# S5 set-up and S5 scans of a hybrid encoder trunk: POOL's share given to DVE, smaller steps, another place for the squares of a norm

## The chip, the cores and the metric

The kernel runs on one core of a Trainium2 chip. The metric is device time in microseconds (us) of one execution, here the median of three runs. The engines are called PE (TensorE, matmuls; PEld are its weight loads), DVE (VectorE), ACT (ScalarE), POOL (GpSimd) and SP (SyncE, which only issues DMAs). Each takes its instructions in order; they meet through semaphores.

## The reference, cut to what matters

The program is a trunk of two layers over 512 tokens of width 1024, all in f32. Layer 0 mixes with RWKV-7 and Mamba-2, layer 1 with an S5 state-space model and an mLSTM, and each layer ends with a squared-ReLU MLP. The change lies in S5, and in what runs beside it. Of S5, per direction, group and state:

```python
dt = exp(log_dt); mag = exp(dt * ar)
abr, abi = mag * cos(dt * ai), mag * sin(dt * ai)        # complex decay of a step
bur = einsum("bsgm,gpm->bsgp", ud, bbr); bui = ...       # inputs, complex
x_t = (abr + i abi) * x_(t-1) + (bur_t + i bui_t)        # a scan over time
yd  = einsum(xr, C_re) - einsum(xi, C_im)
y   = gelu(y); y * sigmoid(y @ glu_w + glu_b)
```

The norm in question is the plain one ahead of layer 1's mixers, `x * rsqrt(mean(x * x) + eps) * w`.

## The kernel before, in words

Every large product is done as three f32r matmuls (`mm3`, `project`, lines 99 to 101 and 112 to 114): the weights come by DMA into `wraw` (SP queue, line 86), ACT rounds them into `whi` (line 87), DVE takes the rest as `wlo` (line 88), and a product of 128 rows over 1024 inputs is 24 matmuls of 512 columns. `wraw`, `whi` and `wlo` have two buffers each, and the PSUM tag `mm` has two banks, so weights are ready at most two products ahead and a third product waits until the bank of the first has been read.

**The MLP of layer 0 and what runs beside it.** `mlp` makes 64 such tiles: 10 up, 8 down, 8 up, 8 down, 8 up, 8 down, 6 up, 8 down. An up tile is evacuated by ACT (`hid`, line 219), POOL and DVE (lines 223 and 224), a down tile by DVE (`evac`, line 251) and POOL (the add into `x`, line 253). After each tile `beside()` takes one turn of a generator, `S5.params`, and ties its instructions behind the tile's last DVE instruction (`issue_after`). So a turn of `params` that puts many instructions on DVE stands between the evacuation of one tile and the `wlo` of a later one.

`params` computes in turn 48 the decay of eight steps as a magnitude and a unit complex number (`unit`, `square`), and from it by repeated squaring its powers 1, 2, 4, 8, 16 and 32; then the tables `cos` and `sin` (128 x 32 groups x 64 chunks): in round i, k = 2^i new columns are the k first ones times a power, by a complex product `cmul` (lines 1455 to 1460, six elementwise instructions: DVE has three, POOL the other three when it is passed as `eng2`, and DVE all six when it isn't). Before, turns 48 and 49 hold three and five squares, turn 50 the rounds k = 1, 2, 4, 8, turn 51 k = 16, turns 52 and 53 the halves of k = 32, turn 54 a copy of `sin` with the sign turned (ACT, line 1599). Turns 43 to 50 are down tiles, 51 to 56 up tiles, 57 to 64 down tiles.

**The norm ahead of layer 1.** `rms_scale` calls `mean_square`: ACT squares the eight `x` (line 140, three buffers `sq`), POOL adds them one by one (line 145, six adds, `sqa`), PE sums over partitions with a matrix of ones (lines 148 and 149). Pools are stacks on two sides of SBUF. On the right, `pre1` (three `sq`, two `sqa`, one `ms`, 2 KB each) lies behind `xn1` and, of the MLP's memory, on tiles of `act0` that are read by matmuls alone. On the left it comes behind `ml_c` and `io_1`, 21,280 bytes in from where the MLP's pool `io0` began (3 `sq`, 2 `sqa`, `ms`, `rstd`, 2 `hid`, 2 `hid2`, 2 `evac` of 2 KB, in this order): its `sq` buffers then lie on the second `hid2` and on both `evac`, its `sqa` and `ms` on `act0`. After `pre1` the pool `s5_a` (S5's matrices `s5_m`, its inputs `s5_ul`) is opened on the right.

**The S5 scans.** PE's order is written by hand here (`manual_schedule`); for the other engines a planner orders the instructions by its own estimate of their times. First come the four S5 columns (written to DRAM as `s5_ud` and read back transposed as `s5_ul`, line 1622, eight DMAs), then the column of the mLSTM's gates, then `dense_steps(S5_STEPS[0])`, a turn of the gates, `dense_steps(S5_STEPS[1])`, and then the turns of `scan` with `S5_STEPS[2]` dense steps after each, and from turn `S5_STEPS[3]` on a turn of the gates too. The gates have 14 turns. A dense step is one k of a projection, three matmuls; sixteen projections of eight steps are in the chain: three `values` (their `wlo` on DVE), eight gated ones (`wlo`, line 88, and a product, line 1101, on POOL), five `values`. For each of four quarters `scan` does, twice, 8 matmuls of 64 columns into a bank `mix0`, two DVE products with `cos` and `sin` (lines 1638, 1639) and a POOL add (line 1640); then four scans on DVE (lines 1643, 1645); then the rotation back: two DVE products, two POOL memsets (lines 1649, 1650), a DVE and a POOL subtraction (lines 1651, 1652).

Of the kernel before, what the change touches and what calls it, by code (L numbers as in the profile page):

```python
# [14 lines left out]
ALU = mybir.AluOpType  # L15
# [251 lines left out]
PREP = (2, 3)  # L267
SPLIT = 6
END = (4, 24)
S5_STEPS = 4, 2, 7, 2, 3  # L270
OUT_STEPS = (0,) * 10 + (0, 1, 1) * 11 + (0,) * 8
NA = 2
DECAY = float(np.exp(-0.5))
# [1055 lines left out]
class S5:  # L1329
# [16 lines left out]
    def params(self, kp, tp):  # L1346
# [226 lines left out]
        def square(o, x, two=2.0):  # L1573
            tt(zq, x, x, M)
            stt(o[:, 1], x[:, 0], two, x[:, 1], M, M)
            tt(o[:, 0], zq[:, 0], zq[:, 1], Sb)
            unit(o)

        unit(z[0])
        square(z[6], z[0])  # L1580
        square(z[0], z[6])
        square(z[1], z[0], sgn)
        yield
        for i in range(1, 6):
            square(z[i + 1], z[i])
        yield

        tr, ti = self.cos, self.sin[:, 0]
        nc.gpsimd.memset(tr[:, :, 0:1], 1.0)
        nc.gpsimd.memset(ti[:, :, 0:1], 0.0)  # L1590
        for i in range(6):
            k = 1 << i
            for G in ([slice(0, 32)] if k < 32 else [slice(0, 16), slice(16, 32)]):
                n = G.stop - G.start
                b = lambda x: z[i + 1][:, x, G].unsqueeze(2).to_broadcast([128, n, k])
                cmul(tr[:, G, k:2 * k], ti[:, G, k:2 * k], tr[:, G, 0:k], ti[:, G, 0:k], b(0), b(1), (128, n, k), nc.gpsimd)
                if k >= 8:
                    yield
        nc.scalar.activation(self.sin[:, 1], ti, AF.Copy, scale=-1.0)
        yield  # L1600
# [15 lines left out]
    def scan(self, kp, wp):  # L1616

        c, nc = self.c, self.c.nc
        self.ul = ul = kp.tile([128, 32, 64], F32, tag="s5_ul", name="s5_ul")
        us = self.ud.rearrange("i (g m) j c -> j m (i g) c", m=16)  # L1620
        for j in range(8):
            nc.sync.dma_start(ul[16 * j:16 * j + 16], us[j])  # L1622
        self.inputs(kp, 6)
        lo, hi = slice(0, 64), slice(64, 128)
        self.X = X = self.sin
        flat = lambda x: x.rearrange("p g c -> p (g c)")
        M = ALU.mult
        for q in range(4):
            G = slice(8 * q, 8 * q + 8)
            w, t = (c.tile(wp, [128, 2, 8, 64], "s5_" + n, 2) for n in ("w", "t"))  # L1630
            for i in (0, 1):
                ps = c.bank("mix0", 2)
                pv = ps.rearrange("p (x g c) -> p x g c", x=2, g=4)
                for x in (0, 1):
                    for g in range(4):
                        nc.tensor.matmul(pv[:, x, g], lhsT=self.mats[2 * q + i][:, g, x], rhs=ul[:, 8 * q + 4 * i + g], start=True, stop=True)
                H, F = slice(4 * i, 4 * i + 4), slice(8 * q + 4 * i, 8 * q + 4 * i + 4)
                nc.vector.tensor_tensor(out=w[:, :, H], in0=pv, in1=self.cos[:, F].unsqueeze(1).to_broadcast([128, 2, 4, 64]), op=M)
                nc.vector.tensor_tensor(out=t[:, :, H], in0=pv[:, ::-1], in1=self.sin[:, :, F], op=M)
                nc.gpsimd.tensor_tensor(out=w[:, :, H], in0=w[:, :, H], in1=t[:, :, H], op=ALU.add)  # L1640
                yield
            for x in (0, 1):
                nc.vector.tensor_tensor_scan(flat(w[lo, x]), flat(self.rc[lo, G]), flat(w[lo, x]), 0.0, M, ALU.add)  # L1643
                rv = lambda v: flat(v)[:, ::-1]
                nc.vector.tensor_tensor_scan(rv(w[hi, x]), rv(self.rc[hi, G]), rv(w[hi, x]), 0.0, M, ALU.add)  # L1645
            t = c.tile(wp, [128, 2, 8, 64], "s5_t", 2)
            nc.vector.tensor_tensor(out=t, in0=w[:, ::-1], in1=self.sin[:, :, G], op=M)
            nc.vector.tensor_tensor(out=w, in0=w, in1=self.cos[:, G].unsqueeze(1).to_broadcast([128, 2, 8, 64]), op=M)
            nc.gpsimd.memset(X[lo, :, G, 0:1], 0.0)
            nc.gpsimd.memset(X[hi, :, G, 63:64], 0.0)  # L1650
            nc.vector.tensor_tensor(out=X[lo, :, G, 1:64], in0=w[lo, :, :, 0:63], in1=t[lo, :, :, 0:63], op=ALU.subtract)
            nc.gpsimd.tensor_tensor(out=X[hi, :, G, 0:63], in0=w[hi, :, :, 1:64], in1=t[hi, :, :, 1:64], op=ALU.subtract)
            yield

    def outputs(self, kp):
# [98 lines left out]
def trunk(tc, ap, out):  # L1754
    nc = tc.nc
    with ExitStack() as ctx:
# [130 lines left out]
        with ExitStack() as left:  # L1887
            s5k = left.enter_context(pool("s5_k"))

            with pool("s5_t", "right") as tp:  # L1890
                feed_forward(X, 0, s5.params(s5k, tp))
            mlc = left.enter_context(pool("ml_c"))
            ml = Mlstm(c, mlc)
            io = left.enter_context(pool("io_1"))
            c.io = io
            w_in = ap["cd_in"]
            with ExitStack() as right:
                xnp = right.enter_context(pool("xn1", "right"))
                with pool("pre1", "right") as pre:
                    c.io = pre  # L1900
                    xn = [c.split(x, xnp, 8, mix_w[1][:, k:k + 1]) for k, x in enumerate(X)]
                    rstd = c.rms_scale(X, io)
                c.io = io
                sa = right.enter_context(pool("s5_a", "right"))
                column = lambda i, use, eng=None: c.project(w_in[i], 128, xn, lambda ps: use(ps, rstd), eng)
                values = [column(4 + i, lambda ps, r, i=i: ml.values(i, ps, r)) for i in range(8)]
                gated = [column(12 + i, lambda ps, r, i=i: ml.outgate(i, ps, r), nc.gpsimd) for i in range(8)]
                dense = chain(values[:3] + gated + values[3:])
                left_over = 128

                def dense_steps(n):
                    nonlocal left_over
                    left_over -= n
                    for _ in range(n):
                        next(dense, None)

                with tc.manual_schedule(engines={nc.tensor.engine}):
                    s5.inputs(sa, 2)
                    for i in range(4):
                        drain(column(i, lambda ps, r, i=i: s5.columns(i, ps, r)))  # L1920
                    with pool("s5_w") as sw, pool("ml_t") as tp:
                        gates = []
                        drain(column(20, lambda ps, r: gates.append(ml.gates(ps, r, tp))))
                        gates, scan = gates[0], s5.scan(sa, sw)
                        next(gates)
                        dense_steps(S5_STEPS[0])
                        next(gates)
                        dense_steps(S5_STEPS[1])

                        for i, _ in enumerate(scan):  # L1930
                            dense_steps(S5_STEPS[2])
                            if i >= S5_STEPS[3]:
                                next(gates, None)
                        for _ in gates:
                            dense_steps(S5_STEPS[4])
                    pools = [left.enter_context(pool("ml_h0"))]
                    heads = [ml.head(h, pools) for h in range(8)]
                    dense_steps(7)
                    together((s5.outputs(sa), 5), (chain(islice(h, FRONT) for h in heads[:AHEAD_HEADS]), FRONT * AHEAD_HEADS), (dense, left_over))
            with pool("mix1", "right") as mixp, pool("ml_y", "right") as yp, pool("ml_h1") as hp:  # L1940
                pools.append(hp)
                y, mixed = [], []

                def beside_heads():
                    for t in s5.finish(yp, s5_vec):
                        mixed.append(c.split(t, mixp, 4))
                        yield
                    yield from project_out(c, X, ap["cd_out_a"], mixed)
                    yield from project_out(c, X, ap["cd_out_b"], y[:4], 0)

                side = beside_heads()
                for i in range(10):
                    for h, n in ((i - 1, 1), (i, 0), (i - 2, 2)):
                        if 0 <= h < 8 and (n or h >= AHEAD_HEADS):
                            for _ in range((FRONT, MIDDLE, 1)[n]):
                                t = next(heads[h])
                            if n == 2:
                                y.append(c.split(t, yp, 8))
                    for _ in range(BESIDE[i]):
                        next(side, None)  # L1960
                drain(side)
                drain(project_out(c, X, ap["cd_out_b"], y[4:], 4))
# [50 lines left out]
```

## Time and profile before

| | us |
|---|---|
| runs | 1829.66, 1825.49, 1831.63 (median 1829.66) |
| profiled execution | 1829.6 |
| its span | 1827.5 |
| PE busy | 1694.1 (93%) |
| DVE busy | 1182.1 (65%) |
| ACT busy | 733.2 (40%) |
| POOL busy | 584.6 (32%) |
| mean granted TensorE clock | 0.973 |

All times within the execution count from the start of the span. A granted clock of 1.00 is 2.4 GHz, and half of it is 1.2 GHz; a matmul of 512 columns starts every 0.23 us at the first and every 0.43 us at the second. Of the work that concerns us, the MLP of layer 0 ends at about 1048 us, the norm of layer 1 at 1067 us, and the S5 scans and the gates fill 1085 to 1213 us. In a timeline row the last bracket is the idle time of the engine just before the instruction and what ended it. "Busy" of DVE and POOL holds the time in which an instruction that has begun waits for the other of the two.

### The profile page before, as it was taken

To read this page: it belongs to the slowest core of one execution; us is meant where nothing else is said; L and a number is where in the kernel's file an instruction comes from. 1 tells how busy PE (TensorE), PEld (TensorE's weight loads), DVE (VectorE), ACT (ScalarE), POOL (GpSimd) and SP (SyncE) were. 2 spreads that over 40 slices of the span, in tenths; PEclk is the share of its full clock that TensorE was granted. 3 is DMA by queue.
4 is the path that set the end of the run, shared out by engine and by line. 5 is a ranking of instruction groups with operands and counts; after the bars stand their busy time and mean duration, and the time that the engine had idled before them with its cause. 6 is when DMAs were issued, how large, how long until landed. Compare 5 with 4: busy or idle time off the path is not lost. (4 is left out here: it accounts for less than half of the span.)

```text
span 1827.5 us, 26365 instructions
## 1 busy us (share of the span) xinstructions
PE 1694.1 (93%) x10124; PEld 1349.3 (74%) x10124; DVE 1182.1 (65%) x2051; ACT 733.2 (40%) x1262; POOL 584.6 (32%) x569
## 2 busy tenths in 40 slices
PE   7989989899899999999996978699889999999997
PEld 5777767687578787777775857578667788888887
DVE  6879796976876476656566657943657745353555
ACT  5635354433634343232322323144756532323243
POOL 4312121300641225566535224530121222222222
PEclk9999999999999999999998998889989999999999
DMA  4230202124302323334351364254222232333342
GB/s 164 79 93 21 65 22 79 30 70 134 121 18 77 93 93 102 105 116 139 106 160 46 113 171 159 87 192 136 86 77 63 87 99 92 103 94 94 102 130 68
DMA packets 90046, 177.40 MB, mean 97 GB/s; under 512 B 32688, under 2 KB 39600, under 8 KB 89792
## 3 DMA queue, kind: packets, MB, share of 16 engines
q1 hardware_dynamic: 82176, 157.32, 28.2%
q0 software_dynamic: 3200, 11.05, 1.8%
q10 hardware_dynamic: 4544, 7.34, 1.1%
q8 instruction: 80, 1.31, 0.3%
q14 instruction: 46, 0.38, 0.1%
HBM read 149.24 MB, written 28.54 MB: 97 GB/s over the span
## 5 line engine op out<-in xcount | busy, mean ns | idle before, releaser
L101 PE MATMUL mm<-act,wlo 128*128 128x512 f32 (+1 forms) x1264 | 483.8, 383 | 15.6 <-DVE wlo L88 15.2
L99 PE MATMUL mm<-act,whi 128*128 128x512 f32 (+1 forms) x1264 | 485.7, 385 | 12.1 <-ACT hid L219 3.1
L100 PE MATMUL mm<-act,whi 128*128 128x512 f32 (+1 forms) x1264 | 482.4, 382 | 0.7 <-DVE act L126 0.5
L87 ACT ACTIVATE whi<-wraw 128x1024 fp32r<-128x1024 f32 (+1 forms) x230 | 227.4, 989 | 561.2 <-PE mm L100 434.2
L88 DVE TENSOR_TENSOR wlo<-wraw,whi 128x1024 fp32r<-128x1024 f32 (+1 forms) x222 | 309.7, 1395 | 166.1 <-ACT whi L87 162.9
L101 PEld LDWEIGHTS mm<-act,wlo 128*128 128x128 f32 x1264 | 239.3, 189 | 66.4 <-DVE wlo L88 21.5
L99 PEld LDWEIGHTS mm<-act,whi 128*128 128x128 f32 x1264 | 239.1, 189 | 62.4 <-ACT hid L219 4.4
L100 PEld LDWEIGHTS mm<-act,whi 128*128 128x128 f32 x1264 | 239.5, 189 | 47.4 <-DVE act L126 1.4
L114 PE MATMUL mm<-act,wlo 128*128 128x512 f32 (+1 forms) x464 | 188.5, 406 | 23.5 <-POOL wlo L88 18.1
L112 PE MATMUL mm<-act,whi 128*128 128x512 f32 (+1 forms) x464 | 205.3, 442 | 3.4 <-DVE pad L77 1.8
L113 PE MATMUL mm<-act,whi 128*128 128x512 f32 (+1 forms) x464 | 186.7, 402 | 0.0
L223 POOL TENSOR_TENSOR hid<-hid 128x512 f32<-128x512 f32 x64 | 94.2, 1473 | 224.8 <-ACT hid L219 220.4
L253 POOL TENSOR_TENSOR x<-x,evac 128x512 f32<-128x512 f32 x56 | 77.7, 1388 | 192.4 <-DVE evac L251 184.4
L114 PEld LDWEIGHTS mm<-act,wlo 128*128 128x128 f32 (+1 forms) x464 | 89.2, 192 | 49.2 <-POOL wlo L88 20.7
L251 DVE TENSOR_TENSOR evac<-mm,rstd 128x512 f32<-128x512 f32 (+1 forms) x72 | 45.3, 629 | 115.9 <-PE mm L101 115.8
L112 PEld LDWEIGHTS mm<-act,whi 128*128 128x128 f32 (+1 forms) x464 | 89.3, 193 | 29.4 <-issue 5.6
L113 PEld LDWEIGHTS mm<-act,whi 128*128 128x128 f32 (+1 forms) x464 | 89.6, 193 | 15.6 <-issue 1.7
L224 DVE TENSOR_TENSOR act<-hid,act 128x512 fp32r<-128x512 f32 x64 | 46.5, 726 | 61.0 <-POOL hid L223 61.0
L77 DVE TENSOR_TENSOR pad<-mm,rstd 128x512 f32<-128x512 f32 x32 | 21.9, 684 | 49.1 <-PE mm L114 49.1
L145 POOL TENSOR_TENSOR sqa<-sqa,sq 128x512 f32<-128x512 f32 (+1 forms) x30 | 38.8, 1294 | 45.1 <-ACT sq L140 43.1
L76 POOL MEMSET pad<- 128x2 f32 x34 | 3.4, 105 | 154.6 <-DVE sh L768 55.3
L1750 DVE TENSOR_TENSOR x<-mm,x 128x512 f32<-128x512 f32 x32 | 22.1, 690 | 40.8 <-PE mm L101 40.8
(561 smaller groups left out, 2876.9 us busy)
## 6 DMA issues: line engine op xcount, KB each, us to landing
wraw<-mlp_w SPq DMA_DIRECT2D x130, 512.0 KB, 3.5
wraw<-ab_in SPq DMA_DIRECT2D x34, 512.0 KB, 3.6
wraw<-cd_in SPq DMA_DIRECT2D x21, 512.0 KB, 3.6
x<-x SPq DMA_DIRECT2D x16, 256.0 KB, 4.4
wraw<-ab_out_b SPq DMA_DIRECT2D x8, 512.0 KB, 3.5
s_cm<-s_sin POOLq DMA_DIRECT2D x8, 512.0 KB, 5.1
s_bm<-s_bt POOLq DMA_DIRECT2D x8, 512.0 KB, 5.0
s_m<-s_bm SPq DMA_DIRECT2D x8, 512.0 KB, 6.2
```

Source lines behind the costliest of these rows:

```text
L87: nc.scalar.activation(hi[:, :cols], raw[:, :cols], AF.Copy)
L88: (eng or nc.vector).tensor_tensor(out=lo[:, :cols], in0=raw[:, :cols], in1=hi[:, :cols].bitcast(F32), op=ALU.subtract)
L99: nc.tensor.matmul(out, lhsT=wh, rhs=xh, start=start and k == 0, stop=False)
L100: nc.tensor.matmul(out, lhsT=wh, rhs=xl, start=False, stop=False)
L101: nc.tensor.matmul(out, lhsT=wl, rhs=xh, start=False, stop=stop and k == n - 1)
L112: nc.tensor.matmul(out, lhsT=wh, rhs=xh, start=k == 0, stop=False)
L113: nc.tensor.matmul(out, lhsT=wh, rhs=xl, start=False, stop=False)
L114: nc.tensor.matmul(out, lhsT=wl, rhs=xh, start=False, stop=k == len(xs) - 1)
L223: nc.gpsimd.tensor_tensor(out=sq, in0=h, in1=h, op=ALU.mult)
L224: last[0] = nc.vector.tensor_tensor(out=lo, in0=sq, in1=hi.bitcast(F32), op=ALU.subtract)
L251: last[0] = nc.vector.tensor_tensor(out=t, in0=ps, in1=r2[:, a:b], op=ALU.mult)
L253: (nc.vector if b - a < T else nc.gpsimd).tensor_tensor(out=x, in0=x, in1=t, op=ALU.add)
```

## The change

Five edits: (1) the chain of squares in `params` gives up its turn five times instead of two; (2) the tables are made by DVE alone, in pieces of at most 256 elements a partition, with a turn after each piece from k = 4 on; (3) in `scan` the adds, one of the two subtractions and the memsets go from POOL to DVE, and there is a turn after each pair of scans, so 20 turns instead of 12; (4) `S5_STEPS` goes with it; (5) `pre1` is opened on the left.

```diff
-S5_STEPS = 4, 2, 7, 2, 3
+S5_STEPS = 8, 8, 4, 4, 3
 ...
         unit(z[0])
         square(z[6], z[0])
+        yield
         square(z[0], z[6])
         square(z[1], z[0], sgn)
         yield
         for i in range(1, 6):
             square(z[i + 1], z[i])
-        yield
+            if i % 2:
+                yield
 ...
             k = 1 << i
-            for G in ([slice(0, 32)] if k < 32 else [slice(0, 16), slice(16, 32)]):
-                n = G.stop - G.start
+            n = min(32, 256 // k)
+            for G in (slice(g, g + n) for g in range(0, 32, n)):
                 b = lambda x: z[i + 1][:, x, G].unsqueeze(2).to_broadcast([128, n, k])
-                cmul(tr[:, G, k:2 * k], ti[:, G, k:2 * k], tr[:, G, 0:k], ti[:, G, 0:k], b(0), b(1), (128, n, k), nc.gpsimd)
-                if k >= 8:
+                cmul(tr[:, G, k:2 * k], ti[:, G, k:2 * k], tr[:, G, 0:k], ti[:, G, 0:k], b(0), b(1), (128, n, k))
+                if k >= 4:
                     yield
 ...
-                nc.gpsimd.tensor_tensor(out=w[:, :, H], in0=w[:, :, H], in1=t[:, :, H], op=ALU.add)
+                nc.vector.tensor_tensor(out=w[:, :, H], in0=w[:, :, H], in1=t[:, :, H], op=ALU.add)
                 yield
             for x in (0, 1):
                 ...
                 nc.vector.tensor_tensor_scan(rv(w[hi, x]), rv(self.rc[hi, G]), rv(w[hi, x]), 0.0, M, ALU.add)
+                yield
 ...
-            nc.gpsimd.memset(X[lo, :, G, 0:1], 0.0)
-            nc.gpsimd.memset(X[hi, :, G, 63:64], 0.0)
+            nc.vector.memset(X[lo, :, G, 0:1], 0.0)
+            nc.vector.memset(X[hi, :, G, 63:64], 0.0)
             nc.vector.tensor_tensor(out=X[lo, :, G, 1:64], in0=w[lo, :, :, 0:63], in1=t[lo, :, :, 0:63], op=ALU.subtract)
-            nc.gpsimd.tensor_tensor(out=X[hi, :, G, 0:63], in0=w[hi, :, :, 1:64], in1=t[hi, :, :, 1:64], op=ALU.subtract)
+            nc.vector.tensor_tensor(out=X[hi, :, G, 0:63], in0=w[hi, :, :, 1:64], in1=t[hi, :, :, 1:64], op=ALU.subtract)
 ...
-                with pool("pre1", "right") as pre:
+                with pool("pre1") as pre:
```

After it the turns of `params` are: 48 and 49 one square (with what came before it) and two; 50, 51 and 52 one, two and two; 53 the rounds k = 1, 2 and 4; 54 k = 8; 55 and 56 the halves of k = 16; 57 to 60 the quarters of k = 32; 61 the copy on ACT. Before, 6 dense steps stand ahead of the scans, 84 among them, 6 in the gates' last turns; after, 16, 80 and none. Both then have 7 dense steps ahead of S5's outputs.

## Rows read from the trace of the kernel before

**Rows 1.** Busy time by stretch: length, PE, PEld, DVE, ACT, POOL, clock, DMA share, GB/s.
```profile
650.00:660.00 10.00, 10.00 (x46) 8.29 (x45) 9.32 (x34) 3.47 (x7) 2.08 (x2) 1.00 0.20 68
700.00:710.00 10.00, 8.00 (x23) 6.34 (x24) 4.77 (x6) 0.25 (x1) 4.30 (x3) 0.66 0.31 107
937.00:1010.00 73.00, 53.75 (x217) 42.36 (x217) 49.41 (x104) 19.50 (x23) 32.38 (x33) 0.91 0.25 79
1085.00:1213.00 128.00, 95.72 (x439) 75.59 (x438) 96.83 (x109) 34.38 (x45) 62.28 (x41) 0.87 0.45 133
```

**Rows 2.** Timeline of DVE, down tiles: start, length, line, operation, [idle before].
```profile
937.32 0.69 DVE L251 TENSOR_TENSOR evac<-mm,rstd 128x512 f32<-128x512 f32 x1 [2.30 <-PE mm L101]
...
1010.30 0.69 DVE L251 TENSOR_TENSOR evac<-mm,rstd 128x512 f32<-128x512 f32 x1 [1.90 <-PE mm L101]
1011.17 2.28 DVE L88 TENSOR_TENSOR wlo<-wraw,whi 128x1024 fp32r<-128x1024 f32 x1 [0.18 <-ACT whi L87]
...
1015.74 0.69 DVE L251 TENSOR_TENSOR evac<-mm,rstd 128x512 f32<-128x512 f32 x1 [1.62 <-PE mm L101]
```

**Rows 3.** Timeline of DVE, the first instruction of two squares that follow each other.
```profile
953.41 0.23 DVE L1376 TENSOR_TENSOR s_zq<-s_z 128x64 f32<-128x64 f32 x1
...
954.86 0.23 DVE L1376 TENSOR_TENSOR s_zq<-s_z 128x64 f32<-128x64 f32 x1
```

**Rows 4.** Timeline of DVE, products of the tables: with 256 and with 512 elements.
```profile
981.45 0.41 DVE L1459 TENSOR_TENSOR s_sin<-s_sin,s_z 128x256 f32<-128x256 f32 x1
...
988.81 0.69 DVE L1459 TENSOR_TENSOR s_sin<-s_sin,s_z 128x512 f32<-128x512 f32 x1 [1.15 <-POOL s_sin L1460]
989.42 1.53 DVE L1455 TENSOR_TENSOR s_sin<-s_cos,s_z 128x512 f32<-128x512 f32 x1
```

**Rows 5.** Timeline of DVE and PE around a `cmul` of 512 elements on DVE alone.
```profile
696.62 0.68 DVE L1455 TENSOR_TENSOR s_sin<-s_fr,c_s_bc 128x512 f32<-128x512 f32 x1
...
700.73 1.22 DVE L88 TENSOR_TENSOR wlo<-wraw,whi 128x1024 fp32r<-128x1024 f32 x1
...
702.00 0.80 PE L101 MATMUL mm<-act,wlo 128*128 128x512 f32 x1 [3.25 <-DVE wlo L88]
```

**Rows 6.** Timeline of ACT and POOL at the norm of layer 1.
```profile
1051.11 0.62 ACT L140 ACTIVATE sq<-x 128x512 f32<-128x512 f32 x1
...
1049.15 1.30 POOL L253 TENSOR_TENSOR x<-x,evac 128x512 f32<-128x512 f32 x1 [3.98 <-DVE evac L251]
...
1050.48 2.21 POOL L145 TENSOR_TENSOR sqa<-sq,sq 128x512 f32<-128x512 f32 x1
1052.76 7.00 POOL L145 TENSOR_TENSOR sqa<-sqa,sq 128x512 f32<-128x512 f32 x5
```

**Rows 7.** Timeline of SP, ACT and PE ahead of the first scan.
```profile
1085.17 9.62 SPq L1622 DMA_DIRECT2D s_ul<-s_ud  x8
1094.89 1.59 SPq L86 DMA_DIRECT2D wraw<-cd_in  x2
...
1101.58 1.06 ACT L87 ACTIVATE whi<-wraw 128x1024 fp32r<-128x1024 f32 x1 [10.63 <-DMA wraw<-cd_in]
...
1100.59 3.65 PE L1636 MATMUL mix<-s_ul,s_m 128*128 128x64 f32 x16 [9.74 <-DMA s_ul<-s_ud]
```

**Rows 8.** Waits, 1085 to 1213: who for whom, us in total, times, longest.
```profile
PE mm L114 <- POOL wlo L88: 18.1, 6, 7.4
```

**Rows 9.** Groups on POOL, 1085 to 1213: count, busy, mean ns, idle before, releasers.
```profile
L1652 POOL TENSOR_TENSOR s_sin<-s_w,s_t 64x1008 f32<-64x1008 f32 x4 | 13.2, 3297 | 2.7 <-DVE ml_small L1157 1.6 <-DVE s_w L1648 1.0
...
L1640 POOL TENSOR_TENSOR s_w<-s_w,s_t 128x512 f32<-128x512 f32 x8 | 12.1, 1514 | 27.7 <-DVE s_t L1639 26.1 <-DVE ml_small L1154 1.5
...
L1649 POOL MEMSET s_sin<- 64x16 f32 x4 | 0.5, 121 | 17.7 <-DVE s_t L1647 10.3 <-DVE ml_small L1154 7.4
```

**Rows 10.** DVE's own subtraction: its group of four, and one that began ahead of POOL's.
```profile
L1651 DVE TENSOR_TENSOR s_sin<-s_w,s_t 64x1008 f32<-64x1008 f32 x4 | 10.9, 2730 | 0.1
...
1207.40 1.20 DVE L1651 TENSOR_TENSOR s_sin<-s_w,s_t 64x1008 f32<-64x1008 f32 x1
```

## The prediction

> **What bounds the kernel now.** I read busy time by stretch first. PE is the engine that everything waits for, so what counts is where it stands still or runs at half clock. Two stretches touch the change. From 937 to 1010 PE is busy 53.75 of 73.00 us at a granted clock of 0.91: 19.25 idle, and 53.75 x 0.09 = 4.8 lost to the clock, 24.0 together. From 1085 to 1213 it is busy 95.72 of 128.00 at 0.87: 32.3 idle and 12.4 of clock, 44.7 together [rows 1]. The timeline of DVE gives the first number once more: from the evacuation at 937.32 (turn 48) to that at 1010.30 (turn 57) there are nine tiles, and one takes 1015.74 - 1010.30 = 5.44 us, so 72.98 - 48.96 = 24.0 [rows 2]. Then the waits and the timelines say who is late: in the first stretch DVE, which holds the squares and half of the tables in front of `evac` and `wlo`; in the second, S5's inputs, for which PE stands still 9.74 us ahead of the first scan matmul [rows 7], and POOL, on whose `wlo` PE waits 18.1 us in six waits [rows 8].
>
> The sum is made against the profiled execution, 1829.6 us (span 1827.5 and 2.1 around it); the median of the runs is 1829.66, so it holds for both.
>
> **Squares and tables (edits 1 and 2).** Removed: nine squares in two turns, and products on two engines that hinder each other. A DVE product of 512 elements takes 0.69 us alone and 1.53 beside POOL's [rows 4]. Added: POOL's three products of each `cmul` on DVE. With 256 elements one takes 0.41 us and the next begins 0.33 later [rows 4], so a piece is at most 6 x 0.41 = 2.5 us. One square is 954.86 - 953.41 = 1.45 us [rows 3], two are 2.9. Turn 53 has eighteen products of 32 to 128 elements, below 0.3 us each: 4 to 5 us. What covers them is the pace of 5.44 us. In a down tile DVE owes 0.69 for `evac` and 2.28 for `wlo` [rows 2], which leaves 2.47: a piece of 2.5 just fits, two squares are 0.4 over. Up tiles have more room: from 650 to 660 DVE is busy 9.32 of 10 us, mostly with strings of small S5 products behind up tiles, and PE 10.00 of 10 at full clock [rows 1]; turn 53 is of that kind. I charge the seven down turns (48 to 50, 57 to 60) 0.6 us each, 4 in all, and so take 24.0 - 4 = **-20.0**. Bounds: -24.0 if all hides; +54 if each of 13 turns costs what the worst one of before costs (rival e). The copy on ACT only moves to a down tile. The splits of `xn`, which lie on the memory of `params`, come up to six tiles later, in the last four tiles of the MLP, where DVE has 2.47 us a tile for them; if that is too little, the first column waits, which I keep in the range.
>
> **The place of the squares (edit 5).** In the trace the first square is written as the MLP's last tile ends, and the POOL chain of six adds begins at 1050.48, just as POOL's last add into `x` (1049.15 and 1.30) is done, and ends at 1059.76 [rows 6]. In the new place the three `sq` lie on both `evac`, which that same add reads. So squares can't all begin ahead of 1050.45; then two of 0.62 us stand ahead of the first add: **+1.2**. Behind ACT's squares is `whi` of the third column, for which PE has no bank before the norm is done. Bounds: if the squares ran under the MLP's last tiles only one add would be left, 9.28 - 1.3 = -8; if ACT's split of the last `x` goes first too, +2. The same edit takes `s5_m` and `s5_ul` off the memory of `pre1`, so S5's loads may start earlier; SP issues the eight `s5_ul` loads over 9.62 us [rows 7], and if they have DMA for themselves the rest of PE's 9.74 us goes as well. I don't count on it.
>
> **More dense steps ahead of the scans.** Ten more steps of three matmuls, 10 x 3 x 5.44 / 24 = 6.8 us, go into the 9.74 us in which PE waits for `s5_ul` [rows 7]. The dense steps in front of S5's outputs are 96 before and after, so nothing else moves: **-6.8**. Bounds: -9.7 if the loads land earlier too; +2.5 if the weights of the second chain stay behind `s5_ul` on SP as now (issued 1094.89, `whi` at 1101.58 [rows 7], `wlo` 1.2 later, so PE, through with the first chain at about 1091, would wait to 1103.8: 12.2 after the gates' transposes). I think that SP takes them earlier, since they are now traced ahead of the scan. The rest of the second chain moves with its matmuls (`wlo`, `pad` and two products on DVE, two passes and two DMAs on ACT), ahead of the first scan product, where DVE has the gates' softplus alone.
>
> **The scans (edit 3).** POOL loses 13.2 + 12.1 + 1.0 = 26.3 us of work, and with it the waits in which its own `wlo` stands behind S5: 17.7 us of idle time ahead of a memset of 0.12, 27.7 ahead of the adds [rows 9]. DVE gains eight adds at 0.69 (the like in [rows 4]), four subtractions at 1.20 [rows 10] and eight memsets at 0.12: 11.3 us on 96.83 busy of 128 [rows 1]. What PE can win is the 18.1 us of waits for POOL's `wlo` and the clock lost behind them. I take half of the 18.1 and 1 us of clock, **-10**, since DVE is then busy nearly throughout and the scan matmuls wait for its banks. Bounds: all 18.1 and half of the clock, -24; the whole 11.3 on PE's path, +11. The gates' turns begin two turns later in count and end before the scans do; their dense steps are in the 96.
>
> A DVE instruction that begins beside a POOL one stretches to POOL's end: its subtraction takes 1.20 us when it goes first and 2.73 in the mean of four [rows 10]. The Trainium skill ("SBUF — State Buffer", "Who interferes with whom") says why: a DVE instruction with two SBUF inputs and a POOL instruction that reads SBUF exclude each other, whichever starts first. By that rule DVE's 96.83 us holds much waiting for POOL, the 26.3 us taken off POOL return more than the 11.3 added, and the scans would come to -24 rather than -10, which is part of rival (a). The rows agree on the exclusion; none shows what the planner's order would make of it.
>
> **Sum.** -20.0 + 1.2 - 6.8 - 10 = -35.6, and 1829.6 - 35.6 = **1794**.
>
> **Rivals.** (a) All of it hides: -24, 0, -9.7, -24: 1772. For it: what [rows 10] show of DVE and POOL, and DVE at 9.32 of 10 us beside an unhindered PE [rows 1]. Against: DVE at more than three quarters of 128 us, with latencies in its chain of product, add, scan and rotation.
> (b) DVE becomes the bound of the scans, and its 11.3 us come on top with nothing won: 1829.6 - 20.0 + 1.2 - 6.8 + 11.3 = 1815. For it: DVE is the busiest engine there after PE. Against: POOL's waits are for DVE to pass work on, and the passing goes away.
> (c) The planner leaves an evacuation behind later `wlo` again, so that one PSUM bank is held, and only a third of the 24 us comes back, -8: 1806. For it: the two evacuations that were late by several tiles in this stretch; against: smaller turns leave less to misplace.
> (d) The second chain's weights stay behind `s5_ul` on SP: +2.5 for -6.8 is 1803. For it: that is their order now [rows 7]; against: the order in which they are traced.
> (e) The other side: `wlo` queued behind table turns. A `cmul` of 512 elements on DVE alone, begun at 696.62 ahead of a `wlo` at 700.73, cost PE a wait of 3.25 us [rows 5], and from 700 to 710 it ran at 0.66 with 8.00 us busy [rows 1], 2.7 of clock: 6.0 a turn. Thirteen such turns are 78 us for the 24 of now, +54: 1829.6 + 54 + 1.2 - 6.8 - 10 = 1868. It decides from (24.0 + 15.6) / 13 = 3.0 us lost a turn on. For it: the same six products in a row on DVE, now in thirteen tiles. Against: the delay there was 4.1 us and is 2.5 at 256 elements, against 2.47 of room.
>
> **How the numbers follow.** Forecast 1794 (its own range 1783 to 1805) 0.45; (a) 0.12; (b) 0.19; (c) 0.10; (d) 0.06; (e) 0.08. The range 1774 to 1820 leaves out about half of (a), the upper part of (b) and (e). A change of 0.3% (5.5 us) is about what a measurement of this kernel can tell from none; within it, 1824 to 1835, lie the tails of (b) and (c), 0.05; above it (e), 0.08; below it 0.87.
>
> **What would show it.** Tables: `cmul` all on DVE, none over 0.5 us an instruction, tiles of turns 48 to 61 at a pace below 5.9 us, the clock at 1.00 there; wrong if PE waits for `wlo` over 1 us in several of them. Norm: POOL's first add of squares at about 1051.7 less what was won before it, and the chain no shorter; wrong if ACT's squares run under the MLP's last tiles. Gap: PE's wait for `s5_ul` below 4 us; wrong if it waits for `wlo` of the second chain. Scans: PE's waits for POOL's `wlo` below 9 us in all, DVE's subtraction near 1.2 us; wrong if PE's waits for `mix` banks or for DVE take their place. The prediction as a whole is wrong if the stretch from the first scan column to S5's outputs is not at least 10 us shorter, or the MLP's end doesn't come 12 us earlier.

## The result, and the profile after

The kernel after takes 1802.35 us (median of four runs, 1800.09 to 1805.26); the kernel before, on the same chip, 1828.93 (four runs, 1825.49 to 1831.63). The ratio is 0.9857, with a 95% interval of 0.9832 to 0.9881: 26.6 us faster. The forecast was 1794, so the time lies 8 us above it, inside the forecast's own range. But the way there was another one in three of four steps.

The profiled execution takes 1804.3 us with a span of 1802.5, 25.0 less than before. Where the 25.0 come from is read off six marks in the timelines (us):

| | before | after | change |
|---|---|---|---|
| start to the evacuation of turn 48 | 937.32 | 940.26 | +2.9 |
| turn 48 to turn 57 (nine tiles) | 72.98 | 65.31 | -7.7 |
| turn 57 to turn 64 | 38.08 | 37.17 | -0.9 |
| last evacuation to the first column's `sh` | 18.97 | 20.00 | +1.0 |
| first column to the gates' column | 18.30 | 18.32 | 0.0 |
| gates' column to S5's first output (`s_cos<-mix` on ACT, `yl` in the kernel) | 142.55 | 120.88 | -21.7 |
| from there to the end | 599.30 | 600.56 | +1.3 |

The first line is the spread of executions: nothing is changed ahead of turn 48, and over all the profiled kernels below this mark lies between 935.3 and 943.2. Two lines carry the gain, and they are not the two that the forecast had in front: -8.6 in the MLP where -20.0 was forecast, -21.7 in the scans where -16.8 was.

Busy time by stretch, in the columns of [rows 1]: the two halves of turns 48 to 57, and the gates and scans.

```profile
940.26:978.83 38.57, 30.80 (x120) 23.94 (x118) 15.69 (x39) 10.63 (x13) 4.53 (x5) 0.91 0.30 97
978.83:1005.57 26.74, 25.49 (x103) 20.30 (x104) 26.41 (x83) 7.95 (x11) 7.59 (x7) 0.94 0.25 77
1081.06:1196.44 115.38, 100.83 (x470) 81.83 (x468) 109.81 (x133) 40.94 (x53) 37.92 (x23) 0.88 0.48 139
```

In the second half DVE is busy 26.41 of 26.74 us with squares, tables and late work, and PE still 25.49: the small steps do hide. The loss is in the first half, where DVE has only 15.69 of 38.57 to do. PE's waits from turn 48 to turn 57 (total, times, longest) say the same. Before, from 937 to 1010:

```profile
PE mm L101 <- DVE wlo L88: 10.7, 1, 10.7
```

and after, from 940 to 1006:

```profile
PE mm L99 <- DVE s_zq L1376: 2.9, 1, 2.9
PE mm L99 <- ACT hid L219: 2.8, 2, 1.4
PE mm L99 <- DVE evac L251: 2.8, 1, 2.8
PE mm L101 <- DVE wlo L88: 0.5, 1, 0.5
```

The first three of these stand in before with the same numbers, 8.5 us in all. So of the 19.2 us that PE stood still in before, 10.7 were a wait for `wlo` behind squares and tables, and the edits took it away; 8.5 were something else, and they stayed. The first is PE's wait for the bank of turn 49, although the row names the small instruction right behind its evacuation; the second are two products of up tiles that wait until ACT has read the bank before them. The timeline of DVE there (start, length, line, operation, idle before) answers [rows 2]:

```profile
940.26 0.69 DVE L251 TENSOR_TENSOR evac<-mm,rstd 128x512 f32<-128x512 f32 x1 [2.30 <-PE mm L101]
...
953.12 0.69 DVE L251 TENSOR_TENSOR evac<-mm,rstd 128x512 f32<-128x512 f32 x1
963.40 1.22 DVE L88 TENSOR_TENSOR wlo<-wraw,whi 128x1024 fp32r<-128x1024 f32 x1 [5.66 <-ACT whi L87]
970.54 1.23 DVE L88 TENSOR_TENSOR wlo<-wraw,whi 128x1024 fp32r<-128x1024 f32 x1 [5.92 <-ACT whi L87]
977.69 1.23 DVE L88 TENSOR_TENSOR wlo<-wraw,whi 128x1024 fp32r<-128x1024 f32 x1 [5.92 <-ACT whi L87]
978.83 0.68 DVE L251 TENSOR_TENSOR evac<-mm,rstd 128x512 f32<-128x512 f32 x1
1005.57 0.68 DVE L251 TENSOR_TENSOR evac<-mm,rstd 128x512 f32<-128x512 f32 x1
```

Turn 50 is evacuated at 978.83, 25.7 us after turn 49, and the three `wlo` in front of it are those of later tiles. DVE stands idle 5.7 to 5.9 us before each: they need `whi`, `whi` needs PE, and PE has one PSUM bank left, since the other holds turn 50. That is the mechanism of rival (c).

The tables' products of 256 elements, by form in 978 to 1030 (count | busy, mean ns): six instructions a piece. Four of the six take 0.41 us in the mean of the seven pieces. The one below doesn't: in three of the seven it meets POOL's add into `x` and takes 1.52 or 1.53 us, so "none over 0.5 us an instruction" did not come true.

```profile
L1456 DVE TENSOR_TENSOR s_sin<-s_sin,s_z 128x256 f32<-128x256 f32 x7 | 6.2, 888 | 0.0
```
```profile
1006.50 1.52 DVE L1456 TENSOR_TENSOR s_sin<-s_sin,s_z 128x256 f32<-128x256 f32 x1
```

The norm, in the view of [rows 6]: the first add of squares begins at 1046.69, 1.9 us after POOL is free (1043.51 and 1.30), and waits for ACT's squares.

```profile
1043.51 1.30 POOL L253 TENSOR_TENSOR x<-x,evac 128x512 f32<-128x512 f32 x1 [3.98 <-DVE evac L251]
1045.47 1.66 ACT L140 ACTIVATE sq<-x 128x512 f32<-128x512 f32 x3
1046.69 1.30 POOL L145 TENSOR_TENSOR sqa<-sq,sq 128x512 f32<-128x512 f32 x1 [1.79 <-ACT sq L140]
```

SP and PE ahead of the first scan, in the view of [rows 7]: the second chain's `wraw` is now issued ahead of `s_ul`, and PE's wait is 1.53 us for 9.74.

```profile
1077.82 0.33 SPq L86 DMA_DIRECT2D wraw<-cd_in  x1
1078.73 11.99 SPq L1624 DMA_DIRECT2D s_ul<-s_ud  x8
...
1094.31 2.00 PE L1638 MATMUL mix<-s_ul,s_m 128*128 128x64 f32 x16 [1.53 <-DMA s_ul<-s_ud]
```

PE's waits from 1081 to 1200, in the view of [rows 8] (total, times, longest): the 18.1 us for POOL's `wlo` are gone, and in their place are two waits for the gates' chain on DVE.

```profile
PE aux L1174 <- DVE ml_li L1164: 10.6, 1, 10.6
PE aux L1182 <- DVE ml_diag L1180: 2.4, 1, 2.4
PE mix L1638 <- DMA s_ul<-s_ud: 1.5, 1, 1.5
```

The groups that answer [rows 9, 10]: POOL's `wlo` waits for ACT alone, and DVE's subtractions take 1.90 and 1.45 us in the mean, not 2.73, but not the 1.20 of [rows 10] either.

```profile
L88 POOL TENSOR_TENSOR wlo<-wraw,whi 128x1024 fp32r<-128x1024 f32 x8 | 20.6, 2570 | 34.9 <-ACT whi L87 34.9
...
L1654 DVE TENSOR_TENSOR s_sin<-s_w,s_t 64x1008 f32<-64x1008 f32 x4 | 7.6, 1899 | 0.1
L1655 DVE TENSOR_TENSOR s_sin<-s_w,s_t 64x1008 f32<-64x1008 f32 x4 | 5.8, 1449 | 0.1
```

### The profile page after: what moved, and what is told of

It reads as the page before. It is cut to its first block, busy times and chain, and to the rows that moved or that the text cites. A ratio compares the mean times of both kernels' runs of the same rounds, so it can differ in the third digit from the quotient of the medians.

```text
span 1802.5 us, 26376 instructions
## 1 busy us (share of the span) xinstructions
PE 1697.4 (94%) x10124; PEld 1355.1 (75%) x10124; DVE 1184.7 (66%) x2110; ACT 733.7 (41%) x1263; POOL 543.7 (30%) x528
## 4 chain that ended last, share of the span: by engine, by line
PE 38%; DVE 8%; ACT 3%; issue 3%; POOL 2%; DMA 0%; DVEq 0%; POOLq 0%; ACTq 0%
PE mm L99 10%; PE mm L100 9%; PE mm L101 9%; PE mm L112 1%; PE mm L113 1%; PE mm L114 1%; DVE wlo L88 1%; DVE s_w L1647 1%; PE mm L1272 1%; POOL hid L223 1%; POOL sqa L145 0%; DVE s_w L1642 0%; ACT whi L87 0%; DVE s_w L1645 0%; PE mm L1277 0%
## 5 line engine op out<-in xcount | busy, mean ns | idle before, releaser
L88 DVE TENSOR_TENSOR wlo<-wraw,whi 128x1024 fp32r<-128x1024 f32 (+1 forms) x222 | 300.4, 1353 | 176.1 <-ACT whi L87 173.4
L253 POOL TENSOR_TENSOR x<-x,evac 128x512 f32<-128x512 f32 x56 | 83.8, 1497 | 184.0 <-DVE evac L251 176.1
```

The costliest lines, as they stand in the source:

```text
L88: (eng or nc.vector).tensor_tensor(out=lo[:, :cols], in0=raw[:, :cols], in1=hi[:, :cols].bitcast(F32), op=ALU.subtract)
L253: (nc.vector if b - a < T else nc.gpsimd).tensor_tensor(out=x, in0=x, in1=t, op=ALU.add)
```

## The experiments

Ratios are to the kernel before on the same chip, with their 95% intervals, those of the experiments from five rounds. The stretches are those of the table above.

| kernel | ratio | 48 to 57 | norm | scans |
|---|---|---|---|---|
| before | 1 | 72.98 | 18.97 | 142.55 |
| after | 0.9857 [0.9832, 0.9881] | 65.31 | 20.00 | 120.88 |
| tables_only | 0.9923 [0.9898, 0.9947] | 65.23 | 19.37 | 139.69 |
| before_tz | 0.9957 [0.9940, 0.9974] | 72.34 | 19.36 | 139.60 |
| tables_tz | 0.9873 [0.9855, 0.9892] | 55.03 | 19.37 | 139.65 |
| after_tz | 0.9786 [0.9770, 0.9801] | 55.06 | 19.98 | 122.08 |
| steps_only | 1.0018 [1.0006, 1.0030] | 75.91 | 19.24 | 143.56 |
| scan_only | 0.9939 [0.9921, 0.9956] | 76.02 | 19.23 | 129.14 |
| norm_only | 0.9992 [0.9979, 1.0004] | 76.07 | 19.59 | 138.44 |
| tz_right | 0.9830 [0.9810, 0.9850] | 55.04 | 19.37 | 129.31 |
| tz_pool | 0.9854 [0.9836, 0.9871] | 54.90 | 19.98 | 132.17 |
| tz_g8 | 0.9814 [0.9792, 0.9836] | 55.06 | 19.99 | 126.12 |
| best | 0.9757 [0.9738, 0.9777] | 51.05 | 21.04 | 126.90 |
| best_ch | 0.9749 [0.9727, 0.9771] | 51.06 | 19.97 | 127.05 |

**The MLP.** Why does turn 50 come late? Ahead of it lie eight DMAs (256 KB each) that turns 46 and 47 issue from POOL's queue. In the timeline of POOL of the kernel after each keeps POOL for 0.62 us, and they stand between POOL's adds into `x`, the instructions that free `evac`:

```profile
930.15 1.29 POOL L253 TENSOR_TENSOR x<-x,evac 128x512 f32<-128x512 f32 x1 [3.16 <-DVE evac L251]
932.72 2.48 POOL L1547 DMA_DIRECT2D s_tz<-s_rm  x4 [1.27 <-DMA s_rm<-s_cos]
935.60 1.29 POOL L253 TENSOR_TENSOR x<-x,evac 128x512 f32<-128x512 f32 x1 [0.40 <-DVE evac L251]
936.82 2.47 POOL L1547 DMA_DIRECT2D s_tz<-s_rm  x4
```

`evac` has two buffers, so if the planner puts the adds of turns 48 and 49 late in its plan, it must put the evacuation of turn 50 behind whatever else is ready. Four kernels cross this cause with the edits 1 and 2.

tables_only is the kernel before with edits 1 and 2. 

> The kernel before with edits 1 and 2 alone (squares and tables). Theory A, one late evacuation: most of the time lost from turn 48 to turn 57 goes with the evacuation of turn 50, which stands behind three later wlo on DVE and does so here as well; 48 to 57 takes about 65 us as in the kernel after (before 73.0), so 7 to 9 us less than before, a ratio of 0.995 to 0.996. Theory B, room on DVE, as in the prediction: the squares and tables themselves made the loss, and in small steps they give 20 us back, a ratio of 0.989.

before_tz and, with the same line, after_tz and tables_tz (edits 1 and 2 and this line):

```diff
-            nc.gpsimd.dma_start(self.tz[16 * j:16 * j + 16], ...)
+            nc.sync.dma_start(self.tz[16 * j:16 * j + 16], ...)
```

> The kernel before with one word changed: the eight small DMAs s5_tz<-s5_rm of turns 46 and 47 are issued by SP and not by POOL; squares and tables stay as they were, on both engines and in big steps. Theory A: these DMAs, spread by the planner over several tiles, hold POOL's adds back in the plan and with them the evacuation of turn 50; without them it is in its place, and of the 24.0 us lost from 48 to 57 at least 10 come back, a ratio of 0.994 or lower. Theory B: the loss comes from the big steps on DVE, so it stays, within 3 us of before, ratio 0.998 to 1.002. A rival of A: SP's weight loads are late behind the DMAs, some us slower than before.

> Edits 1 and 2 and the eight DMAs on SP. Theory A: the loss from 48 to 57 falls to 4 us or less, so 20 us or more under the kernel before, a ratio of 0.989 or lower; what it gains over the kernel before with the DMAs moved alone is what the small steps are worth by themselves, 3 to 10 us. Theory B: nothing beyond edits 1 and 2 alone, ratio as that run's.

> The kernel after with the eight DMAs s5_tz<-s5_rm issued by SP. Theory A: 12 to 16 of the 16.3 us that turns 48 to 57 still lose in the kernel after come back, 1802 to 1788, a ratio to the kernel before of 0.977 to 0.980. Theory B: DVE has no room for the squares in down tiles whoever issues the DMAs, so within 3 us of the kernel after, ratio 0.985 to 0.987.

Measured: tables_only is 14 us faster (0.0077 of 1833), more than theory A's 7 to 9 and less than B's 20; its stretch from 48 to 57 is that of the kernel after, 65.23, as theory A had it. after_tz gives about what A had asked for: 55.06 for 65.31, 9.5 us by the two spans and 13 by the ratios (0.9786 for 0.9857). Its turn 50 is evacuated in place:

```profile
945.24 0.68 DVE L251 TENSOR_TENSOR evac<-mm,rstd 128x512 f32<-128x512 f32 x1
950.51 0.69 DVE L251 TENSOR_TENSOR evac<-mm,rstd 128x512 f32<-128x512 f32 x1 [0.66 <-PE mm L101]
953.48 2.35 DVE L88 TENSOR_TENSOR wlo<-wraw,whi 128x1024 fp32r<-128x1024 f32 x2
```

But before_tz shows that A isn't the whole: there no later `wlo` stands in front of turn 50 either (949.58), and 48 to 57 still takes 72.34. The timelines of its DVE and PE name what is late instead:

```profile
949.58 0.68 DVE L251 TENSOR_TENSOR evac<-mm,rstd 128x512 f32<-128x512 f32 x1
958.34 4.07 DVE L88 TENSOR_TENSOR wlo<-wraw,whi 128x1024 fp32r<-128x1024 f32 x2
```
```profile
960.47 0.80 PE L101 MATMUL mm<-act,wlo 128*128 128x512 f32 x1 [13.90 <-DVE wlo L88]
```

Between the evacuation and `wlo` lie 27 small instructions on DVE, squares and the first rounds of the tables, and PE waits 13.9 us for it, where before it waited 10.7. So the loss of the kernel before has two causes. To take away the big turns alone leaves the late evacuation (65.23). To take away the late evacuation alone leaves the big turns, whose wait grows (72.34). To take away both gives 55.03, more than the two gains together. Both theories were half right. By the run times the gains just about add up, 14 and 8 us alone and 23 together (0.9923, 0.9957, 0.9873); some of that lies outside this stretch, and which part isn't settled. That it is these DMAs that displace the evacuation is shown; that the planner holds them for longer than the 0.62 us they take is argued from where it put them.

**The scans.** steps_only moves dense steps alone, scan_only is the kernel before with edits 3 and 4, norm_only with edit 5.

```diff
-S5_STEPS = 4, 2, 7, 2, 3
+S5_STEPS = 8, 8, 6, 2, 4
```

> The kernel before with S5_STEPS = 8, 8, 6, 2, 4 alone: 16 dense steps ahead of the scans for 6, 72 among the twelve turns for 84, 8 in the gates' last turns for 6; the scans themselves, with POOL's share, as before. Prediction: the 9.74 us wait ahead of the first scan is filled, -6.8 us, a ratio of 0.996. Rival: what is put in front is missing among the scans, where POOL and DVE are the bound, so PE waits longer there by as much, ratio 0.999 to 1.001.

> The kernel before with edits 3 and 4 alone (scans on DVE in 20 turns, S5_STEPS = 8, 8, 4, 4, 3). Prediction: -16.8 us in all, a ratio of 0.991, of which 10 by the scans on DVE. From the stretch between the gates' column and the first S5 output in the kernel after: -19 to -22, ratio 0.988 to 0.990. The part of the scans on DVE is this run less the one with the steps alone.

> The kernel before with edit 5 alone (pre1 on the left). Prediction: +1.2 us in the norm and nothing else, ratio 1.000 to 1.001. Theory of the early inputs: the loads of S5's matrices and inputs come earlier, which is worth 8 us where DVE bounds the scans; here POOL does (18 us of PE's waits), so what PE gains on its 9.7 us wait for s_ul is given back in part, 2 to 7 us faster, ratio 0.996 to 0.999.

steps_only went as its rival had it, a little slower. The wait ahead of the first scan falls by 5.2 us, but POOL's `wlo` takes 1.8 of them back (before: 18.1 in six, the longest 7.4 [rows 8]), PE waits 3.5 us longer for ACT (`ml_tok`, `whi`) and 2.1 less for DVE's `wlo`, and it is busy 3.2 us longer from the gates' column to S5's first output. PE's waits there, from 1087 to 1225:

```profile
PE mm L114 <- POOL wlo L88: 19.9, 4, 11.1
PE mix L1636 <- DMA s_ul<-s_ud: 4.5, 1, 4.5
```

scan_only is 11 us faster (8 to 14), short of both figures expected. Less steps_only, as its expectation has it, the scans on DVE are worth 14 us: 129.14 for 143.56 in the stretch, and as much by the ratios. norm_only can't be told from no change: 1.5 us faster, between 3.8 faster and 0.7 slower. The 1.2 us of the prediction don't show, and of its rival's 2 to 7 all above 4 is excluded.

tz_right is after_tz without edit 5; tz_pool is after_tz with POOL's share of the scans given back:

```diff
-                nc.vector.tensor_tensor(out=w[:, :, H], in0=w[:, :, H], in1=t[:, :, H], op=ALU.add)
+                nc.gpsimd.tensor_tensor(out=w[:, :, H], in0=w[:, :, H], in1=t[:, :, H], op=ALU.add)
...
-            nc.vector.tensor_tensor(out=X[hi, :, G, 0:63], ...)      # and the two memsets
+            nc.gpsimd.tensor_tensor(out=X[hi, :, G, 0:63], ...)
```

> The kernel after with the eight DMAs on SP, and without edit 5 (pre1 again on the right). Prediction: edit 5 costs 1.2 us in the norm, so this one is 0.5 to 1.5 us faster than with edit 5, and PE's wait for s_ul stays below 4 us since ten dense steps cover it. Rival: edit 5 is what lets S5's loads start earlier, and without it PE waits 4 us or more for s_ul, so 2 to 4 us slower.

> The kernel after with the eight DMAs on SP, but POOL has its share of the scans back (adds, one subtraction of two, memsets), with the 20 turns and all the rest as they are. Prediction: the share on DVE is worth 10 us, so about 1804 to 1808, a ratio of 0.984 to 0.986. Theory of the exclusion: DVE waits out each of POOL's instructions, so its stretch gets no shorter by what it gives away, and POOL's wlo are late again: 13 us or more slower than with the share on DVE, ratio 0.986 or higher. Rival: DVE, busy 98% of the stretch, is the bound by its own work, and 11 us less of it make the scans shorter: ratio below 0.976.

tz_right is 8 us slower than after_tz (0.9830 against 0.9786), 7.2 of them in the scans: the rival, and more of it than expected. SP in tz_right, and the second scan product on DVE:

```profile
1068.16 0.90 SPq L1615 DMA_DIRECT2D s_m<-s_bm  x2
1070.67 15.47 SPq L1624 DMA_DIRECT2D s_ul<-s_ud  x8
...
1086.79 7.23 SPq L86 DMA_DIRECT2D wraw<-cd_in  x2
```
```profile
1102.78 0.69 DVE L1640 TENSOR_TENSOR s_w<-mix,s_cos 128x512 f32<-128x512 f32 x1 [6.86 <-PE mix L1638]
```

and the same in after_tz:

```profile
1067.49 0.33 SPq L86 DMA_DIRECT2D wraw<-cd_in  x1
1068.39 12.46 SPq L1624 DMA_DIRECT2D s_ul<-s_ud  x8
```
```profile
1092.51 0.69 DVE L1640 TENSOR_TENSOR s_w<-mix,s_cos 128x512 f32<-128x512 f32 x1
```

Without edit 5 two loads of `s_m` are still in flight when `s_ul` is due; the eight `s_ul` take 15.47 us to issue, and the weights of the dense steps among the first scans stand behind them. Most of the 15.47 is waiting. SP's waits in tz_right, from 1060 to 1100, show that it issues several `s_ul` only once an earlier transfer has landed, one of `s_m` among them:

```profile
SPq L1624 <- DMA s_m<-s_bm: 4.8, 1, 4.8
SPq L1624 <- DMA ml_xc<-sh: 3.2, 1, 3.2
```

Counted from the gates' column (1072.16 and 1070.72) the second product comes at 30.6 us without edit 5 and at 21.8 with it: 8.8 us, about what the scans lose. That is rival (d)'s place and mechanism, met in a kernel without the edit.

tz_pool bears out the prediction's price: 10.1 us longer scans (132.17 against 122.08), 12 us by the ratios. It keeps the 20 turns and the steps that go with them, so this is the price of POOL's share in the new order, not in the old. PE's waits for POOL are back in it, from 1081 to 1200, where the kernel after has none:

```profile
PE mm L114 <- POOL wlo L88: 15.0, 4, 10.1
```

Busy time of both from the gates' column to near the end of the scans, tz_pool first:

```profile
1070.52:1196.00 125.48, 100.38 (x464) 78.71 (x463) 100.97 (x113) 40.72 (x53) 60.22 (x43) 0.89 0.44 127
```
```profile
1070.72:1187.00 116.28, 99.15 (x468) 80.27 (x467) 110.69 (x134) 41.11 (x54) 38.61 (x23) 0.90 0.50 139
```

DVE's busy time grows by 9.7 us when it takes over work for which 11.3 was worked out, so little waiting for POOL was hidden in it. What shrinks is its idle time, 125.48 - 100.97 = 24.5 to 116.28 - 110.69 = 5.6: in this stretch the handing over to POOL and back cost more than the work.

**A faster version.** tz_g8 lets the gates begin four turns of the scans later, so that PE comes later to the transposes for which it waits 10.6 us. best adds to after_tz an empty turn 50, twelve dense steps in front of those transposes, and `wlo` of the last five `values` on POOL. best_ch also moves one copy of the gates from ACT to DVE.

```diff
-S5_STEPS = 8, 8, 4, 4, 3
+S5_STEPS = 8, 8, 4, 8, 3                                    # tz_g8
...
         square(z[1], z[0], sgn)
         yield
+        yield                                               # best, best_ch
...
-                values = [column(4 + i, lambda ps, r, i=i: ml.values(i, ps, r)) for i in range(8)]
+                values = [column(4 + i, lambda ps, r, i=i: ml.values(i, ps, r), nc.gpsimd if i > 2 else None) for i in range(8)]
...
-                            dense_steps(S5_STEPS[2])
+                            dense_steps(S5_STEPS[2] + 12 * (i == 10))
...
-        nc.scalar.activation(self.ch, cm, AF.Copy, scale=-1.0)
+        nc.vector.tensor_scalar(out=self.ch, in0=cm, scalar1=-1.0, scalar2=None, op0=ALU.mult)   # best_ch
```

> The kernel after with the eight DMAs on SP and S5_STEPS[3] = 8 for 4: the gates' turns from the third on stand beside the ninth to twentieth turn of the scans, not beside the fifth to sixteenth. Theory: PE's 10.6 us wait for the gates' chain on DVE comes from PE reaching the transposes too early; 5 to 9 us of it go, a ratio of 0.974 to 0.976 to the kernel before. Rival: DVE, busy 98% of this stretch, is the bound, so the wait moves to the scan matmuls or to the gates' last turns and the time stays, ratio 0.978 to 0.980, or some us slower since the gates' last turns then stand behind the scans.

> The kernel after with the eight DMAs on SP, and three edits more: turn 50 of the tables is left empty (one yield more), so that the wlo behind its evacuation isn't late; 12 dense steps more stand ahead of the transposes for which PE waits 10.6 us; and wlo of the last five values goes from DVE to POOL. Theory: the 6.1 us still lost from turn 48 to 57 fall to 2 to 4; PE's wait for the gates' chain falls below 4 us and 4 to 8 us of dense work are missing behind the scans: 1780 to 1788, ratio 0.971 to 0.976. Rival: DVE bounds the scans, and the added columns put their products on it, so the scans get longer by what is saved later, and only the tables' part shows, ratio 0.977 to 0.980.

> The kernel called best (1787), with one instruction more moved: the copy ml_ch<-ml_cm of the gates is made by DVE and not by ACT, which stood 12.3 us in front of it, waiting for DVE, while the evacuation of a bank for which PE waits 9.1 us stood behind it. Theory of the blocked queue: the 9.1 us go, 3 to 6 us of them show at the end, 1781 to 1785, ratio 0.972 to 0.974. Rival, DVE's own work bounds this stretch: PE waits elsewhere for DVE and the time stays within 2 us of best, ratio 0.975 to 0.977.

tz_g8 is slower than after_tz by some 5 us (0.9814 against 0.9786), its rival. The wait it was to remove went, and another came, for a bank that ACT frees late; in best_ch, where ACT frees it in time, PE waits for the gates' chain again. PE's waits in tz_g8, best and best_ch:

```profile
PE mm L112 <- ACT sh L1100: 8.4, 1, 8.4
```
```profile
PE mm L112 <- ACT sh L1100: 9.1, 1, 9.1
```
```profile
PE aux L1174 <- DVE ml_li L1164: 12.2, 1, 12.2
```

best_ch is no faster than best (1786.8 and 1787.4). In each of the four arrangements, after_tz among them, one large wait is left, while DVE is busy 110.69 of 116.28 us in after_tz and 115.12 of 120.87 in best_ch (below). So DVE's own work seems to set the length of this stretch, and where PE waits only tells where it meets that; no kernel with less work on DVE and no hand-overs was run.

```profile
1064.13:1185.00 120.87, 103.39 (x506) 83.33 (x505) 115.12 (x133) 45.28 (x57) 50.37 (x28) 0.94 0.50 141
```

best beats both kernels, by 18 us the kernel after (0.0100 of 1832; the two were timed on different chips, so the ratios count). Of the 5.1 us between its span and that of after_tz, 4.0 come from the empty turn (55.06 to 51.05): PE's wait for `wlo` of turn 51 falls from 3.9 to 1.5, and the granted clock of the stretch rises from 0.97 to 1.00. The twelve steps, with `wlo` on POOL, make the scans 4.8 longer and the rest of the program 7.2 shorter, 2.4 in all, and the norm takes 1.1 longer.

## Why the prediction was right or wrong

**Squares and tables, -20.0: wrong in size, by rival (c).** The step that failed is "I charge the seven down turns (48 to 50, 57 to 60) 0.6 us each", with all else of the 24.0 taken as won. It named the turn's length as the only cause of the loss. Of PE's 19.2 us, 10.7 were that, and they went (0.5 after); 8.5 stood around two late evacuations, which the text noted as "two evacuations that were late by several tiles" and priced as a rival at 0.10 with -8; measured -7.7 from 48 to 57 and -8.6 with the turns behind. What the steps themselves cost was not far off in sum: with the other cause gone (tables_tz) the loss is 55.03 - 48.96 = 6.1 us, and 57 to 64 loses nothing, for the 4 charged. But it lies in one place, not in seven: 3.9 of it in one wait for `wlo` behind the squares of turn 50, where the text had "two squares are 0.4 over".

**The place of the squares, +1.2: right in kind in the norm, about half in size, and wrong in what it left out.** The norm takes 1.0 us more than before, but before is the lowest of the kernels without the edit (18.97 to 19.37); in the pair that differs in it alone, tz_right and after_tz, it is 0.6, by the step named (the first add waits for ACT's squares). But "S5's loads may start earlier [...] I don't count on it" was the larger part: 8 us between tz_right and after_tz, where the scans are on DVE and ten more steps stand ahead of them, and nothing that can be told from noise in the kernel before (norm_only). Which of the two differences makes it worth 8 us was not tried.

**Ten more dense steps, -6.8: wrong as a term of its own.** The wait was filled as forecast (1.5 us for 9.74, and rival (d) did not come), but alone the steps give nothing (steps_only): "so nothing else moves" failed, since they are missing in the scans, and PE waits and works longer there by as much. What they are worth beside the new scans was not tried.

**The scans, -10: near in size.** It is 10.1 us by tz_pool's stretch and 14 by scan_only less steps_only, by the step named: POOL's waits go, all 18.1 us of them, and DVE takes more than half back, 13.0 in two waits for the gates. That is also the sign by which the text wanted this step called wrong ("for DVE take their place"). Rival (b)'s condition came true as well, DVE busy 109.81 of 115.38 us, but its price did not. From the rule of the Trainium skill ("SBUF — State Buffer", "Who interferes with whom") that a DVE instruction with two inputs in SBUF and a POOL instruction that reads SBUF exclude each other, the prediction worked out that the work taken off POOL would return more than the 11.3 us added, to -24. The trace bears out the exclusion (a product of 256 elements takes 0.41 us and 1.52 beside POOL's add), not that price: of the 11.3 us, 11.3 - 9.7 = 1.6 came back.

Put together: the sum of -35.6 loses 11.4 in the MLP, wins 4.9 in the scans, and the two unchanged ends of this execution add 4.2: -25. In the scans the terms went +1.0 for the steps, -14.4 for DVE's share with its 20 turns and about -8 for edit 5, where -6.8, -10 and 0 stood. These are errors of both signs, and that the time came out inside the forecast's own range is in good part luck. Of the two conditions that the prediction set for itself, one held (the scans 10 us shorter: 21.7) and one failed (the MLP's end 12 us earlier: 5.6), so by its own words the prediction as a whole is wrong.

## What to carry to other kernels

One lost stretch can have two causes, and a change aimed at one leaves the other: split PE's standstill by wait first, and read what is late once more with the first cause gone, before the whole loss is booked as a gain. Where a planner writes the order, look at small instructions on the queue that frees a buffer, not only at long ones on the busy engine; here one word on eight DMAs was worth 8 to 13 us (before_tz to before, after_tz to after). And a gain at the head of a chain needn't arrive at its end: the same edit gave nothing measurable in one kernel and 8 us in another.

## What the runs showed that was not expected

From turn 48 to 57 the profile of before took 72.98 us, and those of the three other kernels that leave the MLP alone 75.9 to 76.1, with DVE, POOL, SP and PE in the same order. The difference is PE's clock. From turn 49's evacuation to turn 50's PE did the same 72 matmuls at a granted clock of 1.00 (2.4 GHz throughout) in before and of 0.87 (a part of it at 1.2 GHz) in the others, and stood still as long (5.7 us); the kernel after has 0.87 there too. Before, and then steps_only:

```profile
950.18:973.05 22.87, 17.18 (x72) 13.28 (x72) 12.47 (x40) 5.94 (x9) 2.62 (x4) 1.00 0.22 70
```
```profile
948.35:973.97 25.62, 19.94 (x72) 15.35 (x72) 11.74 (x40) 5.94 (x9) 3.16 (x4) 0.87 0.20 62
```

So the loss in [rows 2] is 24 to 27 us, depending on the execution, and the edits' gain there 7.7 to 10.7. What made the clock differ is not shown. The scans have such a spread too: tables_only, before_tz and tables_tz leave them alone and took 139.6 to 139.7 us there for the 142.55 of before, so that some 3 of the 21.7 us may not be the edits'. The cause of that is open.

And the same eight `s_ul` loads take SP 9.62 us to issue in before [rows 7], 11.99 in after, 12.46 in after_tz and 15.47 in tz_right. It is not the `s_m` loads as such: two of them stand directly in front in before too, and there no `s_ul` but the first has to wait for a landing. In tz_right five more do, 11.6 us in all: 4.8 for `s_m`, 5.2 for the `ml_xm` and `ml_xc` of the dense steps that now come first, and 1.6 for earlier `s_ul`.
